# Down projection in 1024-column groups, with Strassen's seven products for seven pairs of contraction tiles

## The chip, the cores and the metric

The kernel runs on one core of one Trainium2 chip. The metric is the device time of one execution in microseconds, lower is better. The time before is 1343.54 us, the median of three runs (1343.22 to 1344.33). Engine names in the profile: PE is TensorE (matmul), PEld its weight load, DVE is VectorE, ACT is ScalarE, POOL is GpSimd, SP is SyncE, which issues most loads.

## The reference

One layer of an encoder trunk over 256 positions of width 2048, float32: a parallel mixer (gated MLP and neighbourhood attention), then a convolutional gated MLP, then a final norm. The change touches only the last matrix product of the MLP and what follows it:

```python
D_MODEL = 2048; SEQ = 256; D_FF = 5504; RMS_EPS = 1e-6

def conv_ffn(x, g_norm, w_up, conv_k, conv_b, w_down):
    h = rms_norm(x, g_norm)
    up = h @ w_up
    ...
    gate, val = jnp.split(up, 2, axis=-1)
    return x + (jax.nn.silu(gate) * val) @ w_down

def reference(...):
    for l in range(DEPTH):
        x = mixer_block(...)
        x = conv_ffn(...)
    return rms_norm(x, norm_final)
```

The down projection multiplies 256 x 5504 activations by a 5504 x 2048 weight, 43 contraction tiles of 128.

## The kernel before

**Precision.** All large products keep float32 accuracy with a faster matmul format. Each operand is split into a high part (rounded) and a low part (the rest), and a product is three matmuls that accumulate into one PSUM bank: high x high, low x high, high x low (`products`, L198 to L200). In the down projection the activations are the stationary operand, 128 x 128, and the weights move, 512 columns at a time. The high parts are made by ScalarE (L127), the low parts by VectorE (L128).

**Pieces.** `plan` cuts every weight matrix of the kernel into pieces, in one list for the whole program. In the down projection a piece is two contraction tiles by 512 columns (512 KB), the last one of each group a single tile. Piece by piece, `begin(i)` does three things: it issues loads up to piece i + 4 (SyncE's queue, L104, into five raw tiles `wraw`); it issues the split of piece i + 3 (`split_to`; four buffers each of `whi` and `wlo`, so the split of i + 3 takes the buffers of i - 1 and waits for TensorE to have read them); and it runs the tasks that were put down for turn i with `at(i, f)`. Then the matmuls of piece i are issued. The order is written out by hand: each engine executes its instructions in the order in which this program issues them. A raw tile is free for the next load once both splits have read it.

**The down projection** runs in four groups of 512 output columns (`natural`, `run_group`). A group has 22 pieces; both blocks of 128 positions are done for each piece, 6 matmuls per block and contraction pair, 12 a piece, into two PSUM banks. When a group ends, `ev_down` adds the two banks to the residual `x2` (VectorE, L752), sums the squares (ScalarE, L753), and multiplies with the final norm's weight (VectorE, L762). The weight of the final norm, `gfin`, is loaded in four parts by GpSimd's queue (L943), two buffers. The last group does its last four pieces block by block, so that `finish` of the first block of positions (the norm factor, five scalings, five stores; L777 to L795) runs beside the second block's matmuls.

**Ahead of it** stands the up projection (`ev_up`: convolution, gate, split of the activations; L717 to L738 and L328, L329), whose last tasks fall into the first pieces of the down projection. The activations lie in 43 tiles `a0` to `a42`, the normed input of the up projection in sixteen tiles `h0` to `h15` of a pool that lives to the end.

Of the kernel before, what the change touches and what calls it, by code (L numbers as in the profile page):

```python
# [15 lines left out]
T = 256  # L16
# [23 lines left out]
LOAD_AHEAD = 5  # L40
SPLIT_AHEAD = 3
WAKE = (9, 8)


@with_exitstack
def trunk_kernel(ctx, tc, x, norm_mix, w_in, ln_g, ln_b, w_s, b_s, rpb, w_branch, w_out,
# [30 lines left out]
    def plan(src, row0, nk, blocks):  # L77
        first = len(pieces)
        for k in range(0, nk, 2):
            pieces.append((src, row0 + k * 128, min(2, nk - k), blocks))  # L80
        return first

    raw, split_t = {}, {}
    n_loaded = [0]
    n_split = [0]
    first = {}

    def load_to(n):
        while n_loaded[0] < min(n, len(pieces)):
            i = n_loaded[0]  # L90
            n_loaded[0] += 1
            if i in preload:
                for f in preload[i]:
                    f()
            src, r0, kn, (c0, cn, nb, cs) = pieces[i]
            w = wpool.tile([128, 2, 512], F32, name="wraw", bufs=LOAD_AHEAD)
            ld = src.shape[-1]
            if i == 0:
                for k in range(kn):
                    if k:  # L100
                        load_x(256, 256)
                    nc.sync.dma_start(w[:, k, :cn], src[r0 + k * 128:r0 + (k + 1) * 128, c0:c0 + cn])
            elif nb == 1:
                nc.sync.dma_start(  # L104
                    w[:, :kn, :cn],
                    bass.AP(tensor=src.tensor, offset=src.offset + r0 * ld + c0,
                            ap=[[ld, 128], [128 * ld, kn], [1, cn]]))
            else:
                for b in range(nb):
                    nc.sync.dma_start(  # L110
                        w[:, :kn, b * cn:(b + 1) * cn],
                        bass.AP(tensor=src.tensor, offset=src.offset + r0 * ld + c0 + b * cs,
                                ap=[[ld, 128], [128 * ld, kn], [1, cn]]))
            raw[i] = w

    def split_to(n):
        while n_split[0] < min(n, len(pieces)):
            i = n_split[0]
            n_split[0] += 1
            src, r0, kn, (c0, cn, nb, cs) = pieces[i]  # L120
            w = raw.pop(i)
            h = wpool.tile([128, 2, 512], F32R, name="whi", bufs=SPLIT_AHEAD + 1)
            l = wpool.tile([128, 2, 512], F32R, name="wlo", bufs=SPLIT_AHEAD + 1)
            m = cn * nb

            def part(k):
                nc.scalar.activation(h[:, k, :m], w[:, k, :m], AF.Copy)  # L127
                nc.vector.tensor_sub(l[:, k, :m], w[:, k, :m], h[:, k, :m].bitcast(F32))  # L128
# [73 lines left out]
    def run_group(g, by_block=0):  # L202
        kind, n0, nk, m, acts, done = g
        nblk = NT if kind == "nat" else m // 128
        n1 = n0 + (nk + 1) // 2
        ps = None
        for i in range(n0, n1 - by_block):
            begin(i)
            h, l = split_t.pop(i)
            if ps is None:  # L210
                ps = [bank() for _ in range(nblk)]
            if kind == "ws":
                spread_products(g, ps, i, h, l)
                continue
            for b in range(nblk):
                if b == 1 and i in midway:
                    midway.pop(i)()
                products(g, ps, i, b, h, l)
        if not by_block:
            done(ps, n1)  # L220
            return
        for b in range(nblk):
            for i in range(n1 - by_block, n1):
                if b == 0:
                    begin(i)
                products(g, ps, i, b, *split_t[i])
            done(ps, b)

    def finish_tasks():
        i = cur[0] + 1  # L230
# [100 lines left out]
    xT = [hpool.tile([128, 2, T], F32R, name=f"h{k}") for k in range(KD)]  # L331

    def x_chunk(c):
        p = bank()
# [359 lines left out]
    def turn_x2(j):  # L694
        x2 = rs["x2"]
        for k2 in range(2):
            p = bank()
            for kk in range(2):
                c = j * 4 + k2 * 2 + kk
                for t in range(NT):  # L700
                    nc.tensor.transpose(p[:, kk * T + t * 128:kk * T + (t + 1) * 128],  # L701
                                        x2[:, t, c * 128:(c + 1) * 128], ident)
            k = j * 4 + k2 * 2
            for kk in range(2):
                rs["h", k + kk] = hpool.tile([128, 2, T], F32R, name=f"h{k + kk}")
            split_pair(p, (rs["h", k], rs["h", k + 1]), gffn[:, k:k + 2])


# [37 lines left out]

    fin = {}

    def add_down(ps, t, j):
        x2 = rs["x2"]  # L750
        c = slice(j * 512, (j + 1) * 512)
        nc.vector.tensor_add(x2[:, t, c], ps[t], x2[:, t, c])  # L752
        nc.scalar.activation(junk, x2[:, t, c], AF.Square, accum_out=fin["ss"][:, t, j:j + 1])  # L753

    def ev_down(j):
        def done(ps, i):
            for t in range(NT):
                add_down(ps, t, j)
            x2 = rs["x2"]
            for t in range(NT):  # L760
                c = slice(j * 512, (j + 1) * 512)
                nc.vector.tensor_mul(x2[:, t, c], x2[:, t, c], fin["g", j])  # L762
            if j < 2:
                fin["load"]()
        return done

    def finish_start():
        fin["part"] = const.tile([128, NT], F32, name="part")
        nc.vector.tensor_reduce(fin["part"], fin["ss"][:, :, 0:3], axis=AX.X, op=OP.add)
        nc.vector.tensor_scalar(fin["part"], fin["part"], 1.0 / D, RMS_EPS, op0=OP.mult, op1=OP.add)  # L770

    def finish(ps, t):
        x2 = rs["x2"]
        last = slice(1536, 2048)
        add_down(ps, t, 3)
        y = hpool.tile([128, 512], F32, name=f"h{t}")
# [142 lines left out]
    rs["st"].close()  # L919
    fa, fa_st = pool("act")  # L920
    ctx.push(fa_st)
    ff["a"] = [fa.tile([128, 2, T], F32R, name=f"a{k}") for k in range(NF)]
    fc = {}

    def open_conv():
# [18 lines left out]
                                                 ap=[[0, 128], [1, 512]]))  # L944

    fin["load"] = load_fin
    at(g_dn[3][1], sqrt_ready)
    at(g_dn[3][1] + 2, finish_start)
    for g in g_dn[:3]:
        run_group(g)  # L950
    run_group(g_dn[3], SPLIT_AHEAD + 1)
    finish_tasks()


# [26 lines left out]
```

## Time and profile before

| | |
|---|---|
| median of three runs | 1343.54 us |
| profiled execution | 1342.71 us, span 1340.8 us |
| TensorE busy | 1329.1 us, 99% of the span |
| VectorE busy | 871.2 us, 65% |
| ScalarE busy | 718.6 us, 54% |
| loads of the down weight | 84 of 512 KB and 4 of 256 KB, medians 4.6 and 3.3 us to landing |
| granted TensorE clock, mean | 0.998 |

The span runs from the first to the last instruction. In rows of groups come line, engine, operation, out<-in, shape and count, then after the bar the busy time in us and the mean of one in ns, then the idle time of that engine ahead of these instructions and what ended it. In rows of the timeline come the start and the duration in us, and in brackets the idle time ahead and what ended it; "x2" means that two instructions were merged in the row. Matmuls overlap: the duration of one is its latency, and the pace has to be read from starts. In rows of waits come the total, the number and the longest.

### The profile page before, as it was taken

The page shows a single profiled execution, that of the slowest core. Times are in us where ns is not written, and L with a number is a line of the kernel's source. Part 1 is how long each engine was busy: PE and PEld are TensorE (multiplying, and loading weights), DVE is VectorE, ACT ScalarE, POOL GpSimd, SP SyncE. Part 2 cuts the span into 40 slices and gives each one's busy share as a digit, 9 for nine tenths or more (in the row PEclk, how much of TensorE's full clock was granted, in tenths as well). Part 3 has the DMA queues.
Part 4 walks back from the last instruction along what each step waited for, and adds up shares of the span by engine and source line. Part 5 has one row for each costly group of instructions (what it writes and reads, how often), then busy time and mean ns, then how long its engine had stood idle before and what let it go on. Part 6 is the DMA issues. An engine that isn't in the chain of part 4 may idle for free.

```text
span 1340.8 us, 18983 instructions
## 1 busy us (share of the span) xinstructions
PE 1329.1 (99%) x6863; PEld 1128.8 (84%) x6863; DVE 871.2 (65%) x1256; ACT 718.6 (54%) x1059; POOL 104.4 (8%) x192
## 2 busy tenths in 40 slices
PE   9999999999999999999999999999999999999997
PEld 7888888888888888888888888888888888888885
DVE  6486667766564545555777777777777785545454
ACT  6655566667544444455655555555555554434342
POOL 0241055530000000000000000000000000000000
PEclk9999999999999999999999999999999999999999
DMA  9766685654666666665565656665665557666662
GB/s 328 224 191 177 202 232 172 193 172 157 204 187 189 190 189 220 204 203 185 178 196 181 193 184 191 187 189 188 188 190 187 174 175 227 210 184 210 187 200 100
DMA packets 194030, 259.36 MB, mean 193 GB/s; under 512 B 12952, under 2 KB 124432, under 8 KB 193936
## 3 DMA queue, kind: packets, MB, share of 16 engines
q1 hardware_dynamic: 189648, 250.31, 59.6%
q0 software_dynamic: 3968, 7.30, 2.3%
q8 instruction: 54, 0.88, 0.3%
q10 hardware_dynamic: 320, 0.53, 0.1%
q14 instruction: 40, 0.33, 0.1%
HBM read 253.90 MB, written 2.10 MB: 191 GB/s over the span
## 4 chain that ended last, share of the span: by engine, by line
PE 98%; ACT 1%; DVE 0%; DMA 0%; issue 0%; SPq 0%; DVEq 0%; ACTq 0%
PE bank L177 30%; PE bank L198 17%; PE bank L200 17%; PE bank L199 17%; PE bank L181 15%; PE bank L563 1%; DMA wraw<-in_w_in_dram 0%; PE bank L613 0%; PE bank L439 0%; PE bank L659 0%; PE bank L603 0%; PE bank L701 0%; PE bank L338 0%; ACT L634 0%; DVE x L791 0%
## 5 line engine op out<-in xcount | busy, mean ns | idle before, releaser
L128 DVE TENSOR_TENSOR wlo<-wraw,whi 128x1024 fp32r<-128x1024 f32 (+1 forms) x473 | 570.6, 1211 | 397.0 <-ACT whi L127 381.5
L127 ACT ACTIVATE whi<-wraw 128x1024 fp32r<-128x1024 f32 (+1 forms) x473 | 491.4, 1044 | 411.0 <-PE bank L199 279.8
L177 PE MATMUL bank<-h,whi 128*128 128x512 f32 x1760 | 478.6, 395 | 0.0
L177 PEld LDWEIGHTS bank<-h,whi 128*128 128x128 f32 x1760 | 302.2, 189 | 41.5
L181 PEld LDWEIGHTS bank<-h,wlo 128*128 128x128 f32 x1760 | 267.2, 189 | 35.7
L181 PE MATMUL bank<-h,wlo 128*128 128x256 f32 x1760 | 276.7, 281 | 0.0
L198 PE MATMUL bank<-whi,h 128*128 128x512 f32 x384 | 152.5, 397 | 0.1
L199 PE MATMUL bank<-whi,h 128*128 128x512 f32 x384 | 149.9, 390 | 0.3 <-DVE h L325 0.3
L200 PE MATMUL bank<-wlo,h 128*128 128x512 f32 x384 | 150.0, 391 | 0.0
L199 PE MATMUL bank<-whi,a 128*128 128x512 f32 x344 | 133.8, 389 | 0.0
L200 PE MATMUL bank<-wlo,a 128*128 128x512 f32 x344 | 133.8, 389 | 0.0
L198 PE MATMUL bank<-whi,a 128*128 128x512 f32 x344 | 133.8, 389 | 0.0
L200 PEld LDWEIGHTS bank<-wlo,h 128*128 128x128 f32 x384 | 72.2, 188 | 15.7 <-DVE wlo L128 0.4
L199 PEld LDWEIGHTS bank<-whi,h 128*128 128x128 f32 x384 | 72.3, 188 | 14.8 <-DVE h L325 0.6
L198 PEld LDWEIGHTS bank<-whi,h 128*128 128x128 f32 x384 | 72.3, 188 | 14.8 <-ACT whi L127 0.7
L727 ACT ACTIVATE tc<-ta,ck 128x256 f32<-128x256 f32 x86 | 47.1, 595 | 69.8 <-DVE ta L725 69.8
L200 PEld LDWEIGHTS bank<-wlo,a 128*128 128x128 f32 x344 | 64.6, 188 | 13.5
L199 PEld LDWEIGHTS bank<-whi,a 128*128 128x128 f32 x344 | 64.6, 188 | 13.4
L198 PEld LDWEIGHTS bank<-whi,a 128*128 128x128 f32 x344 | 64.6, 188 | 13.3
L943 POOL DMA_DIRECT2D gfin<-in_norm_final_dram x4 | 2.2, 548 | 646.5 <-DVE tc L738 539.2
L730 DVE SCALAR_TENSOR_TENSOR tc<-ta,ck,tc 128x255 f32<-128x255 f32 x86 | 41.4, 481 | 14.4 <-ACT tc L727 14.4
L198 PE MATMUL bank<-whi,m 128*128 128x512 f32 x128 | 50.1, 392 | 0.0
(157 smaller groups left out, 1093.8 us busy)
## 6 DMA issues: line engine op xcount, KB each, us to landing
wraw<-in_w_up_dram SPq DMA_DIRECT2D x336, 256.0 KB, 3.2
wraw<-in_w_in_dram SPq DMA_DIRECT2D x111, 512.0 KB, 4.3
wraw<-in_w_down_dram SPq DMA_DIRECT2D x84, 512.0 KB, 4.6
wraw<-in_w_in_dram SPq DMA_DIRECT2D x66, 256.0 KB, 3.1
wraw<-in_w_branch_dram SPq DMA_DIRECT2D x32, 512.0 KB, 4.5
wraw<-in_w_out_dram SPq DMA_DIRECT2D x32, 512.0 KB, 3.9
xs<-in_x_dram SPq DMA_DIRECT2D x8, 256.0 KB, 7.4
vw<-va POOLq DMA_DIRECT2D x32, 64.0 KB, 5.4
```

Source lines behind the costliest of these rows:

```text
L127: nc.scalar.activation(h[:, k, :m], w[:, k, :m], AF.Copy)
L128: nc.vector.tensor_sub(l[:, k, :m], w[:, k, :m], h[:, k, :m].bitcast(F32))
L177: nc.tensor.matmul(p, h[:, k - k0, b * 128:(b + 1) * 128], acts(k), start=k == 0, stop=k == nk - 1)
L181: nc.tensor.matmul(p[:, :T], l[:, k - k0, b * 128:(b + 1) * 128], acts(k)[:, 0, :], start=False, stop=False)
L198: nc.tensor.matmul(p, xh, h[:, kk, :m], start=st, stop=False)
L199: nc.tensor.matmul(p, xl, h[:, kk, :m], start=False, stop=False)
L200: nc.tensor.matmul(p, xh, l[:, kk, :m], start=False, stop=sp)
L563: nc.tensor.matmul(o, Q[s][:, c], k.rearrange("p (r c) -> p r c", r=ROWS)[:, :, k0:k0 + UNION], start=n == 0, stop=n == 1)
L727: nc.scalar.activation(v, u, AF.Identity, scale=ck[:, 1, ch:ch + 1], bias=ck[:, 3, ch:ch + 1])
L730: nc.vector.scalar_tensor_tensor(v[:, 1:], u[:, :T - 1], ck[:, 0, ch:ch + 1], v[:, 1:], op0=OP.mult, op1=OP.add)
L943: nc.gpsimd.dma_start(fin["g", j], bass.AP(tensor=norm_final.tensor, offset=norm_final.offset + j * 512, ap=[[0, 128], [1, 512]]))
```

## The change

The down projection is done in two groups of 1024 columns. A piece is now one contraction tile by 1024 columns (`plan_wide`), 43 pieces a group, still 512 KB and 12 matmuls (two position blocks x two column halves x three). Four PSUM banks hold a group's outputs (C).

Seven pairs of contraction tiles in each group (`DOWN_QUADS`) are done otherwise. Such a pair is a product of 2 x 2 blocks: position blocks x contraction tiles, times contraction tiles x column halves. It takes seven block products instead of eight: three of them use sums of weights and sums of activations, one uses a sum of activations, one a sum of weights. Three of the seven go into the outputs directly; four are gathered over all seven pairs in four further PSUM banks (P) and are added to the outputs once, at the end of the group's pairs (`ev_sums`).

For a pair whose pieces are i and i + 1 the tasks are:

- at turn i - 3, `act_sums`: VectorE forms float32 activations from high and low (512 columns) and four sums over 128 columns each; ScalarE copies them as high parts, VectorE takes the low parts;
- at turn i - 2, `weight_sums`: four sums over 512 columns from the raw weights, on VectorE;
- at turn i - 1, `weight_sums_split`: two splits over 1024 columns, on ScalarE and VectorE.

The ordinary split of piece i covers only its first 512 columns. The sums lie in the pool of `h`, whose sixteen tiles become eight of double size, with one buffer each; the activations `a` are laid in pairs too.

At the end of group one, `ev_down` adds four banks, and the columns of the final norm are multiplied at the next two turns. The last group does its last four pieces in four steps, by position block and column half; `finish` now also adds the first half's columns and multiplies them.

```diff
+DOWN_QUADS = (2, 5, 7, 10, 12, 15, 17)
...
-            if i:
+            if i in whole:
+                whole[i] = w
+                part(slice(0, units[i]))
+            elif i:
                 part(slice(0, kn))
...
+    def triple(p, x, h, l, st, sp):
+        xh, xl = x
+        nc.tensor.matmul(p, xh, h, start=st, stop=False)
+        nc.tensor.matmul(p, xl, h, start=False, stop=False)
+        nc.tensor.matmul(p, xh, l, start=False, stop=sp)
+
+    def act_sums(g, q, box):
+        a = g[4](q)
+        w = hpool.tile([128, 2, 512], F32, name="h6")
+        f = w[:, 0].rearrange("p (k t) -> p k t", k=2)
+        nc.vector.tensor_add(f, a[:, :, 0, :].bitcast(F32), a[:, :, 1, :].bitcast(F32))
+        s1, s2, s3, s4 = (w[:, 1, n * 128:(n + 1) * 128] for n in range(4))
+        nc.vector.tensor_add(s1, f[:, 0, 128:], f[:, 1, 128:])
+        nc.vector.tensor_sub(s3, f[:, 0, :128], f[:, 0, 128:])
+        nc.vector.tensor_sub(s2, s1, f[:, 0, :128])
+        nc.vector.tensor_sub(s4, f[:, 1, :128], s2)
+        o = hpool.tile([128, 2, 512], F32R, name="h7")
+        nc.scalar.activation(o[:, 0], w[:, 1], AF.Copy)
+        nc.vector.tensor_sub(o[:, 1], w[:, 1], o[:, 0].bitcast(F32))
...
+
+    def weight_sums(i, box):
+        r0, r1 = whole.pop(i), whole.pop(i + 1)
+        t13 = hpool.tile([128, 2, 512], F32, name="h0")
+        t24 = hpool.tile([128, 2, 512], F32, name="h1")
+        nc.vector.tensor_sub(t13[:, 0], r0[:, 1], r0[:, 0])
+        nc.vector.tensor_sub(t24[:, 0], r1[:, 1], t13[:, 0])
+        nc.vector.tensor_sub(t13[:, 1], r1[:, 1], r0[:, 1])
+        nc.vector.tensor_sub(t24[:, 1], r1[:, 0], t24[:, 0])
+        box["w"] = (t13, t24)
+
+    def weight_sums_split(box):
+        u = []
+        for n, t in enumerate(box.pop("w")):
+            h = hpool.tile([128, 2, 512], F32R, name=f"h{2 + n}")
+            l = hpool.tile([128, 2, 512], F32R, name=f"h{4 + n}")
+            nc.scalar.activation(h, t, AF.Copy)
+            nc.vector.tensor_sub(l, t, h.bitcast(F32))
+            u.append((h, l))
...
+        for q in quads:
+            i, b = n0 + 2 * q, boxes.setdefault(q, {})
+            at(i - 3, lambda q=q, b=b: act_sums(g, q, b))
+            at(i - 2, lambda i=i, b=b: weight_sums(i, b))
+            at(i - 1, lambda b=b: weight_sums_split(b))
...
+            if r == 0:
+                (h0, l0), (h1, l1) = split_t[i], split_t[i + 1]
+                triple(P[0], x_of(k, 0), h0[:, 0], l0[:, 0], st, sp)
+                triple(C[0][0], x_of(k + 1, 0), h1[:, 0], l1[:, 0], False, False)
+                triple(C[0][1], boxes[q]["s"][3], h1[:, 1], l1[:, 1], False, False)
...
+            S, W = boxes[q]["s"], boxes[q]["t"]
+            triple(P[1], S[0], *W[1], st, sp)
+            triple(P[3], S[2], *W[3], st, sp)
+            triple(P[2], S[1], *W[2], st, sp)
+            triple(C[1][0], x_of(k, 1), *W[4], False, False)
+            if sp:
+                done[0](P, i)
...
+            def first_half():
+                ...
+                nc.scalar.activation(ab[:, 0], p1, AF.Copy)
+                nc.vector.tensor_add(x11, p1, x11)
+                nc.vector.tensor_add(ab[:, 1], p6, ab[:, 0])
+                nc.vector.tensor_add(m["v"], p5, ab[:, 1])
+                nc.vector.tensor_add(m["u3"], p7, ab[:, 1])
+                m["w"] = ab[:, 0]
+                nc.vector.tensor_add(m["w"], p5, m["u3"])
+
+            def second_half():
+                nc.vector.tensor_add(x12, x12, m["v"])
+                nc.vector.tensor_add(x21, x21, m["u3"])
+                nc.vector.tensor_add(x22, x22, m["w"])
...
-    g_dn = [natural(w_d, 0, NF, j * 512, 512, lambda k: ff["a"][k], ev_down(j) if j < 3 else finish) for j in range(4)]
+    g_dn = [wide(w_d, 0, NF, g * 1024, lambda k: ff["a"][k], lambda q: ff["ap"][q], DOWN_QUADS,
+                 (ev_sums(2 * g), ev_down if g == 0 else finish)) for g in range(2)]
...
+    run_wide(g_dn[0], False)
+    run_wide(g_dn[1], True, SPLIT_AHEAD + 1)
```

More of the change, by code (lines that the diff above doesn't have):

```diff
@@ L79, in plan, with plan_wide @@
         for k in range(0, nk, 2):
-            pieces.append((src, row0 + k * 128, min(2, nk - k), blocks))
+            pieces.append((src, row0 + k * 128, min(2, nk - k), blocks, 128 * src.shape[-1]))
+        return first
+    def plan_wide(src, row0, nk, c0):
+        first = len(pieces)
+        for k in range(nk):
+            pieces.append((src, row0 + k * 128, 2, (c0, 512, 1, 0), 512))
         return first
     raw, split_t = {}, {}
+    whole, units = {}, {}
     n_loaded = [0]
@@ L227, in run_group, with wide @@
             done(ps, b)
+    def wide(src, row0, nk, c0, acts, pair, quads, done):
+        n0 = plan_wide(src, row0, nk, c0)
+        for q in quads:
+            i = n0 + 2 * q
+            whole[i] = whole[i + 1] = None
+            units[i], units[i + 1] = 1, 2
+        return ("wide", n0, nk, acts, pair, quads, done)
+    def triple(p, x, h, l, st, sp):
[3 more added lines that the diff above has]
+        nc.tensor.matmul(p, xh, l, start=False, stop=sp)
@@ L763, in done, with finish @@
-            if j < 2:
-                fin["load"]()
-        return done
+                scale_columns(t, j)
+            fin["load"]()
+        for j in range(2):
+            at(i + 1 + j, lambda j=j: columns(j))
     def finish_start():
         fin["part"] = const.tile([128, NT], F32, name="part")
-        nc.vector.tensor_reduce(fin["part"], fin["ss"][:, :, 0:3], axis=AX.X, op=OP.add)
+        nc.vector.tensor_reduce(fin["part"], fin["ss"][:, :, 0:2], axis=AX.X, op=OP.add)
         nc.vector.tensor_scalar(fin["part"], fin["part"], 1.0 / D, RMS_EPS, op0=OP.mult, op1=OP.add)
-    def finish(ps, t):
+    def finish(ps, t, c):
```

112 lines of the change are left out of this document (89 added, 23 removed).

## The prediction

> **What bounds the kernel now.** I read the head of the page first, then its chain that ended last, then the groups of the down projection, the table of stretches over that stage, and last the timeline of single queues there.
>
> ```profile
> span 1340.8 us, 18983 instructions
> PE 1329.1 (99%) x6863; PEld 1128.8 (84%) x6863; DVE 871.2 (65%) x1256; ACT 718.6 (54%) x1059; POOL 104.4 (8%) x192
> PE 98%; ACT 1%; DVE 0%; DMA 0%; issue 0%; SPq 0%; DVEq 0%; ACTq 0%
> ```
>
> TensorE makes 98% of the chain, so a matmul taken away is worth its pace, as long as every other engine keeps up. The down projection stands at the end:
>
> ```profile
> 1097.84 0.39 PE L198 MATMUL bank<-whi,a 128*128 128x512 f32 x1
> 1331.55 0.39 PE L200 MATMUL bank<-wlo,a 128*128 128x512 f32 x1
> L198 PE MATMUL bank<-whi,a 128*128 128x512 f32 x344 | 133.8, 389 | 0.0
> 1134.20:1161.40 27.20, 27.20 (x122) 22.52 (x121) 14.12 (x14) 11.45 (x15) 0.54 (x1) 1.00 0.58 183
> ```
>
> The first two lines are the first and the last of 3 x 344 = 1032 matmuls: 233.71 us for 1031 steps, 0.2267 us each; the 389 ns of the group are latency, not pace. The last line is one stretch of ten pieces (columns: length, then busy time of PE, PEld, DVE, ACT, POOL, granted clock, DMA share, GB/s): PE is full at clock 1.00, VectorE busy 14.1 of 27.2 us, ScalarE 11.5. A piece is 12 matmuls, 2.72 us. What paces the other two queues:
>
> ```profile
> 1228.38 1.06 ACT L127 ACTIVATE whi<-wraw 128x1024 fp32r<-128x1024 f32 x1 [1.66 <-PE bank L199]
> 1229.48 1.23 DVE L128 TENSOR_TENSOR wlo<-wraw,whi 128x1024 fp32r<-128x1024 f32 x1 [1.49 <-ACT whi L127]
> ```
>
> ScalarE's split of a piece waits 1.66 us for TensorE's last read of the piece whose buffer it takes (four buffers: piece j+3 takes that of j-1), and VectorE waits for ScalarE. So VectorE cannot build up more lead than these buffers. That is what the change meets.
>
> **The change, part by part.** Durations for the new work:
>
> ```profile
> L128 DVE TENSOR_TENSOR wlo<-wraw,whi 128x1024 fp32r<-128x1024 f32 x79 | 96.6, 1226 | 102.5 <-ACT whi L127 102.2
> L762 DVE TENSOR_TENSOR x<-x,gfin 128x512 f32<-128x512 f32 x6 | 4.2, 692 | 0.8 <-ACT junk L753 0.6
> L738 DVE TENSOR_TENSOR tc<-tc 128x256 f32<-128x256 f32 x1 | 0.4, 421 | 0.0
> L783 DVE TENSOR_SCALAR e<-e 128x1 f32<-128x1 f32 x2 | 0.3, 155 | 0.1
> L752 DVE TENSOR_TENSOR x<-bank,x 128x512 f32<-128x512 f32 x8 | 5.2, 685 | 4.1 <-PE bank L200 4.1
> L127 ACT ACTIVATE whi<-wraw 128x1024 fp32r<-128x1024 f32 x79 | 83.4, 1059 | 111.1 <-PE bank L199 111.1
> L127 ACT ACTIVATE whi<-wraw 128x512 fp32r<-128x512 f32 x4 | 2.5, 632 | 6.6 <-PE bank L199 6.6
> 1102.90 2.36 DVE L128 TENSOR_TENSOR wlo<-wraw,whi 128x1024 fp32r<-128x1024 f32 x2
> 1101.74 2.01 ACT L127 ACTIVATE whi<-wraw 128x1024 fp32r<-128x1024 f32 x2
> 1098.38 0.48 DVE L730 SCALAR_TENSOR_TENSOR tc<-ta,ck,tc 128x255 f32<-128x255 f32 x1
> 1098.89 0.48 DVE L732 SCALAR_TENSOR_TENSOR tc<-ta,ck,tc 128x255 f32<-128x255 f32 x1
> ```
>
> Two independent VectorE splits take 2.36 us, not 2 x 1.226: each occupies the queue 0.09 us less than its duration, so 1.14 us for 1024 columns and 0.60 for 512. On ScalarE it is 0.10 (2.01 against 2 x 1.06). An op that needs the one before starts 0.03 after its end (1098.38 + 0.48 to 1098.89). Between engines I take 0.04 (ScalarE's 1228.38 + 1.06 to VectorE's 1229.48). The trace has no plain add or subtract over 128 columns; its bounds are 155 ns (one column) and 421 (256). I take 0.285, the line through 256 and 512 columns (0.421 - 0.136).
>
> The Trainium skill, VectorE: DVE Perf Modes, section The DRAIN you can't avoid, says that after a VectorE op the next one does not start until the pipeline is empty. The 2.36 us above disagree. By that rule there would be no 0.09 to save; the sum would be that of rival B.
>
> *Products.* A quad is two pieces, i and i+1, that are computed by seven products of three matmuls each. Fourteen quads (seven a group, two groups) do 21 matmuls each instead of 24: 42 fewer x 0.2267 = -9.5 us. All of it is on the path.
>
> *VectorE's list for one quad*, queue time, in the order that it is issued: the half split of piece i, 0.60; the sums of activations, 0.73 + 0.20 + 0.20 + 0.32 + 0.32 = 1.77 with the hand-over, then ScalarE's copy 0.63 + 0.04 while VectorE stands, then their low part; behind that copy on ScalarE stands the split of piece i+1 (1.06 us), so VectorE's half of it starts 3.40 after the first sum; 1.14 for it; four sums of weights 0.73 + 3 x 0.60 = 2.53; their two splits 2 x 1.14 = 2.28. Together 0.60 + 3.40 + 1.14 + 2.53 + 2.28 = 9.95 us, against 2.28 for two pieces before. Each plain piece stays 1.14.
>
> *Against TensorE.* Quads begin 4 or 6 pieces apart. Four apart: TensorE has 45 matmuls, 10.20 us; VectorE 9.95 + 2.28 = 12.23: TensorE stands 2.03 us. Six apart: 69 matmuls, 15.64, against 14.51: 1.1 to spare, which cannot be banked, since VectorE then waits for a buffer. From that buffer (TensorE's end of piece i-4, 0.19 until seen) to the first low weights: 0.19 + 0.67 + 0.60 + 3.40 + 1.14 + 2.53 + 1.14 (split of i+2) + 1.27 = 10.94 us; TensorE gets there after 47 matmuls, 10.65: it stands 0.3 to 0.4. So each pair of quads costs 2.4 us, three pairs a group, two groups: 14.4.
>
> *First quad of each group.* It is like six apart, 0.4, but VectorE comes to it late. In group one, with the tail of the up projection:
>
> ```profile
> 1096.37 0.75 DVE L725 TENSOR_TENSOR ta<-ta,rb 128x256 f32<-128x256 f32 x2
> 1099.29 1.22 DVE L128 TENSOR_TENSOR wlo<-wraw,whi 128x1024 fp32r<-128x1024 f32 x1
> 1100.43 0.42 DVE L738 TENSOR_TENSOR tc<-tc 128x256 f32<-128x256 f32 x1
> 1100.76 1.22 DVE L128 TENSOR_TENSOR wlo<-wraw,whi 128x1024 fp32r<-128x1024 f32 x1
> ```
>
> One convolution holds VectorE from 1096.37 to 1099.29, 2.9 us, gate and split 0.33 each: 3.6, in all 4.0. In group two four evictions and four multiplications, 8 x 0.60 = 4.8, in all 5.2 (ScalarE's squares lie beside). Sum of stalls 14.4 + 9.2 = 23.6 us.
>
> *Sums out of PSUM* (five of 0.685 and three of 0.692 a group, and a copy on ScalarE): at nothing. They come in the last seven or eight plain pieces, where VectorE has 2.72 - 1.14 = 1.6 us to spare each. Without that cover 2 x 5 = 10 us.
>
> *Wait for the old sums.* Four apart, ScalarE's copy into the sums' tile also waits until TensorE has read the old ones, and the split of i+1 and VectorE's half of it stand behind. Laid out as above, TensorE is done 2.7 us before; nothing.
>
> *Loads and banks.*
>
> ```profile
> wraw<-in_w_down_dram SPq DMA_DIRECT2D x84, 512.0 KB, 4.6
> wraw<-in_w_down_dram SPq DMA_DIRECT2D x4, 256.0 KB, 3.3
> SPq L104 <- DVE wlo L128: 165.2, 75, 3.9
> ```
>
> SyncE's queue issues 86 loads instead of 84 + 4. It waits for VectorE to free a raw tile before nearly each load (75 times in this stage, 3.9 us at most), and will go on doing so. A quad's two raw tiles are held until the weight sums, two pieces longer, and the load that takes their place starts then; it lands 4.6 us later, near the end of piece i+1, when the split asks for it. Up to 0.1 a quad, taken as nothing. All eight PSUM banks are in use; group two's product banks were group one's output banks, evicted 10 us before their first matmul; nothing. GpSimd's two late loads of the final weights have some 100 us (40 pieces). ScalarE gets 0.63 + 2 x 1.06 more a quad and a half split less, 7 x 2.3 = 16 us a group, and is busy 11.5 of 27.2 us now: not a bound by itself, only by its order behind the copy.
>
> *Tail.*
>
> ```profile
> 1327.21 0.69 DVE L752 TENSOR_TENSOR x<-bank,x 128x512 f32<-128x512 f32 x1 [3.63 <-PE bank L200]
> 1327.94 0.63 ACT L753 ACTIVATE junk<-x 128x512 f32<-128x512 f32 x1 [5.08 <-DVE x L752]
> 1331.00 0.55 DVE L791 TENSOR_SCALAR x<-h,r,e 128x512 f32<-128x512 f32 x1
> 1331.97 0.69 DVE L752 TENSOR_TENSOR x<-bank,x 128x512 f32<-128x512 f32 x1 [0.42 <-PE bank L200]
> ```
>
> The finish of the first row block holds VectorE 4.3 us (1327.21 to 1331.55). Now another block's add, square, multiplication and small op (0.72 + 0.67 + 0.60 + 0.2, about 2.2) come behind it, before the last add: 6.5 us after, while TensorE ends after 24 matmuls, 5.4: +1.0.
>
> **Sum:** -9.5 + 23.6 + 1.0 = +15.1 us. The profiled execution took 1342.71 (span 1340.8 and 1.9 around it), 0.8 under the median of the three runs, 1343.54. Against it 1357.8, against the median 1358.6, which I give.
>
> **Rivals.** *A, the new work hides, faster.* If VectorE's list of a quad took 10.20 - 2.28 = 7.9 us or less, not 9.95, TensorE would hardly stand: -9.5 + 1.0, 1335.0. For it: VectorE is half idle on average. Against: even without both stands for ScalarE (1.1 us) the list is 8.9, and its rows are of the same shapes.
>
> *B, VectorE ops don't overlap.* 24 ops of each ten pieces lose 0.09 us: 2.2 x 6 pairs, +13, 1372. Against: the 2.36 us.
>
> *C, the clock falls in the stalls.* At its start the kernel shows slow matmuls:
>
> ```profile
> 7.11 0.63 PE L199 MATMUL bank<-whi,h 128*128 128x512 f32 x1
> 7.53 0.48 PE L200 MATMUL bank<-wlo,h 128*128 128x512 f32 x1
> ```
>
> 0.42 us apart, not 0.227. If both first quads, where TensorE stands 4 to 5 us with pauses, led to 15 such matmuls each, +5.8, 1364.4. Against: the single stands are 1.3 to 2.9 us. The Trainium skill, TensorE: Matmul & The Clock Gate, Part 1, has the clock halved after an idle window of about 3.4 us; no run here shows such a window, and by it a single stand would not do.
>
> *D, the spare time is banked.* If VectorE kept the 1.1 us of the six-apart stretches, a pair would cost 0.9: stalls 5.4 + 9.2, in all +6.1, 1349.6. Against: the 1.66 us wait for the buffer.
>
> **Chances.** Forecast 0.72, A 0.08, B 0.07, C 0.05, D 0.08. The 128-column ops alone move the sum: at 0.155 the four take 0.5 us less a quad, 14 x 0.5 = 7 down; at 0.42 as much up. With D and hand-overs shorter by 0.02 the low end is 1346; B gives the high end, 1372. A stays outside. Within 0.2% of before (2.7 us, about what a measurement can tell): 0.02, from D with cheap sums; faster 0.08, A; slower 0.90.
>
> **What would show it.** PE's matmuls of the stage: 990 at an unchanged 389 ns. The first use of the summed weights should wait for their high and low parts, 2 us in quads four apart, 0.4 in six, 4 to 5 in first ones; TensorE otherwise waits for nothing. VectorE is over 90% busy from piece 1 to 36 of each group, granted clock 1.00. If VectorE idles there for buffers, A holds; a row of two splits in 2.45 us shows B.

## The result, and the profile after

The changed kernel takes 1366.38 us, the median of four runs (1363.70 to 1366.78); the kernel before, beside it, 1343.38 (1342.94 to 1344.33). The ratio is 1.0166, with a 95% interval of 1.0154 to 1.0179: 23.0 us slower. The profiled execution took 1366.30, span 1364.3, against 1340.8 before: 23.5 us to explain.

The head of its page, the granted clock by slices, the chain that ended last, and the loads of the down weight:

```profile
span 1364.3 us, 19137 instructions
PE 1332.9 (98%) x6821; PEld 1123.4 (82%) x6821; DVE 967.6 (71%) x1440; ACT 744.6 (55%) x1101; POOL 104.5 (8%) x192
...
PEclk9999999999999999999999999999999989998999
...
PE 90%; DVE 6%; ACT 2%; issue 1%; DMA 0%; SPq 0%; ACTq 0%; DVEq 0%
...
wraw<-in_w_down_dram SPq DMA_DIRECT2D x86, 512.0 KB, 5.3
```

Forty-two matmuls are gone (6863 before, 6821 now), yet TensorE is busy 3.8 us longer. Eight points of the chain that were TensorE's are now VectorE's, ScalarE's and "issue". Two slices of the clock row have an 8, where the row of before has a 9 throughout. So there are two things to look for: places where TensorE stands, and matmuls that are themselves slow.

TensorE in the timeline (start, duration, then the idle time ahead and what ended it): the first and last matmul of the stage, the first quad of group one, one pair of stands four pieces apart, and the first wait of group two:

```profile
1098.95 0.39 PE L253 MATMUL bank<-whi,a 128*128 128x512 f32 x1
...
1112.06 0.50 PE L253 MATMUL bank<-whi,a 128*128 128x512 f32 x1 [1.38 <-ACT whi L135]
...
1113.32 0.50 PE L255 MATMUL bank<-wlo,a 128*128 128x512 f32 x1 [0.53 <-DVE wlo L136]
...
1116.34 0.79 PE L253 MATMUL bank<-h,h 128*128 128x512 f32 x1 [1.83 <-ACT h L287]
...
1118.45 0.80 PE L255 MATMUL bank<-h,h 128*128 128x512 f32 x1 [0.90 <-DVE h L288]
...
1122.87 0.40 PE L253 MATMUL bank<-whi,a 128*128 128x512 f32 x1
...
1146.89 0.50 PE L253 MATMUL bank<-h,h 128*128 128x512 f32 x1 [0.48 <-ACT h L287]
...
1148.61 0.50 PE L255 MATMUL bank<-h,h 128*128 128x512 f32 x1 [0.99 <-DVE h L288]
...
1242.38 0.79 PE L253 MATMUL bank<-h,h 128*128 128x512 f32 x1 [2.91 <-ACT h L287]
...
1353.82 0.39 PE L255 MATMUL bank<-wlo,a 128*128 128x512 f32 x1
```

The stage has 990 matmuls and lasts 254.87 us from the first start to the last, against 233.71 for 1032 before: +21.16. At the old pace 989 steps would take 224.2, so 30.7 us are lost. I took each step between two starts and put down what it has above 0.2267 us to the place where it stands. Between 1118.45 and 1122.87 no matmul waits, but ten steps take 4.42 us instead of 2.27; the first takes 0.60 us and the others 0.41 to 0.43 each. Told apart in this way, standing and slow matmuls make:

| where (group one, group two) | lost | of it slow matmuls |
|---|---|---|
| first quad of group one | 8.3 | 2.0 |
| first quad of group two | 6.8 | 2.3 |
| six quads four apart | 2.01, 2.02, 2.06, 2.06, 2.07, 3.65 | 1.6 in the last figure |
| six quads six apart | 0.17 to 0.19 each, 1.1 in all | none |
| all else | 0.6 | none |

Against that stand 42 x 0.2267 = 9.5 us saved. From the start of the last matmul to the end of the span it is 10.49 us instead of 9.22: +1.3. The stage began 1.1 us later (1098.95 against 1097.84). Matched matmul by matmul, the two traces are already 1.1 us apart from about 207 us on, 890 us ahead of the stage; and in the profiles of the experiments the stage begins anywhere from 1097.95 to 1099.39: it is spread between executions. 21.16 + 1.27 + 1.11 = 23.5.

Windows of the stage (columns as in the prediction: length, busy time of PE, PEld, DVE, ACT, POOL, granted clock, DMA share, GB/s):

```profile
1108.00:1118.00 10.00, 5.82 (x20) 3.35 (x18) 8.91 (x16) 5.60 (x8) 0.57 (x1) 0.90 0.20 67
1118.00:1128.00 10.00, 9.54 (x33) 7.73 (x34) 7.00 (x11) 3.01 (x4) 0.55 (x1) 0.76 0.96 304
1139.07:1167.23 28.16, 26.69 (x116) 21.16 (x115) 24.64 (x35) 14.14 (x16) 0.00 (x0) 1.00 0.59 202
...
1298.00:1308.00 10.00, 8.48 (x30) 6.19 (x29) 9.49 (x12) 4.96 (x5) 0.00 (x0) 0.83 0.61 186
```

The second line is the plain case of "busy but slow": TensorE 9.54 us busy, 33 matmuls instead of 44, clock 0.76. The third is VectorE's cycle of ten pieces with two quads. It lasts 28.16 us, while TensorE has 114 matmuls in it (10 x 12, less 2 x 3), 25.84 us at the old pace.

What VectorE does in that cycle, with the last convolution of the up projection and the first sum of group one ahead of it, and the tail behind it:

```profile
1105.74 0.75 DVE L857 TENSOR_TENSOR ta<-ta,rb 128x256 f32<-128x256 f32 x2
...
1108.66 0.68 DVE L261 TENSOR_TENSOR h<-a 128x512 f32<-128x512 f32 x1
...
1141.58 0.69 DVE L269 TENSOR_TENSOR h<-h,h 128x512 fp32r<-128x512 f32 x1 [0.78 <-ACT h L268]
1142.53 1.23 DVE L136 TENSOR_TENSOR wlo<-wraw,whi 128x1024 fp32r<-128x1024 f32 x1 [0.26 <-ACT whi L135]
...
1147.34 2.35 DVE L288 TENSOR_TENSOR h<-h,h 128x1024 fp32r<-128x1024 f32 x2
...
1154.41 0.69 DVE L136 TENSOR_TENSOR wlo<-wraw,whi 128x512 fp32r<-128x512 f32 x1 [1.31 <-ACT whi L135]
...
1353.11 0.68 DVE L884 TENSOR_TENSOR x<-bank,x 128x512 f32<-128x512 f32 x1
...
1355.32 0.68 DVE L884 TENSOR_TENSOR x<-bank,x 128x512 f32<-128x512 f32 x1
```

VectorE stands 0.78 + 0.26 us in a quad behind ScalarE's copy, and 1.31 us once in this cycle because the split it needs waits for a buffer. The rest is a full list. Groups and waits of the stage:

```profile
L269 DVE TENSOR_TENSOR h<-h,h 128x512 fp32r<-128x512 f32 x14 | 9.7, 693 | 10.3 <-ACT h L268 10.3
...
L253 PE MATMUL bank<-whi,a 128*128 128x512 f32 x260 | 101.8, 392 | 1.4 <-ACT whi L135 1.4
...
L263 DVE TENSOR_TENSOR h<-h 128x128 f32<-128x128 f32 x14 | 4.1, 292 | 0.5
```

```profile
PE bank L253 <- ACT h L287: 7.8, 8, 2.9
PE bank L255 <- DVE h L288: 7.4, 8, 1.0
```

TensorE's sixteen waits for summed weights make 15.2 us: eight for the high parts, and after each of these one for the low parts, in the two first quads and the six quads four apart.

### The profile page after: what moved, and what is told of

It is laid out like the page before. It is cut to its first block, busy times and chain, and to the rows that moved or that the text cites. A ratio compares the mean times of both kernels' runs of the same rounds, so it can differ in the third digit from the quotient of the medians.

```text
span 1364.3 us, 19137 instructions
## 1 busy us (share of the span) xinstructions
PE 1332.9 (98%) x6821; PEld 1123.4 (82%) x6821; DVE 967.6 (71%) x1440; ACT 744.6 (55%) x1101; POOL 104.5 (8%) x192
## 4 chain that ended last, share of the span: by engine, by line
PE 90%; DVE 6%; ACT 2%; issue 1%; DMA 0%; SPq 0%; ACTq 0%; DVEq 0%
PE bank L188 30%; PE bank L192 15%; PE bank L209 10%; PE bank L211 10%; PE bank L210 10%; PE bank L255 4%; PE bank L253 4%; PE bank L254 4%; DVE wlo L136 2%; ACT whi L135 1%; DVE h L288 1%; PE bank L696 1%; DVE h L277 0%; DVE h L279 0%; DMA wraw<-in_w_in_dram 0%
## 5 line engine op out<-in xcount | busy, mean ns | idle before, releaser
L136 DVE TENSOR_TENSOR wlo<-wraw,whi 128x1024 fp32r<-128x1024 f32 (+1 forms) x471 | 560.3, 1198 | 315.0 <-ACT whi L135 301.1
L135 ACT ACTIVATE whi<-wraw 128x1024 fp32r<-128x1024 f32 (+1 forms) x471 | 482.0, 1033 | 341.9 <-PE bank L210 164.0
L253 PE MATMUL bank<-whi,a 128*128 128x512 f32 x260 | 101.8, 392 | 1.4 <-ACT whi L135 1.4
L255 PE MATMUL bank<-wlo,a 128*128 128x512 f32 x260 | 101.3, 390 | 0.5 <-DVE wlo L136 0.5
L254 PE MATMUL bank<-whi,a 128*128 128x512 f32 x260 | 101.4, 390 | 0.0
L209 PEld LDWEIGHTS bank<-whi,h 128*128 128x128 f32 x384 | 72.3, 188 | 15.1 <-ACT whi L135 0.9
L253 PEld LDWEIGHTS bank<-whi,a 128*128 128x128 f32 x260 | 49.2, 189 | 12.1 <-ACT whi L135 1.8
L255 PEld LDWEIGHTS bank<-wlo,a 128*128 128x128 f32 x260 | 49.0, 189 | 11.4 <-DVE wlo L136 1.1
L254 PEld LDWEIGHTS bank<-whi,a 128*128 128x128 f32 x260 | 49.1, 189 | 10.3
```

The lines of the kernel that those rows point to most:

```text
L209: nc.tensor.matmul(p, xh, h[:, kk, :m], start=st, stop=False)
L253: nc.tensor.matmul(p, xh, h, start=st, stop=False)
L254: nc.tensor.matmul(p, xl, h, start=False, stop=False)
L255: nc.tensor.matmul(p, xh, l, start=False, stop=sp)
```

## The experiments

All edits are against the changed kernel; the kernel before was run beside each. My theory was that VectorE's list is too long for quads four apart and for a first quad that starts too early, that six apart it fits, and that slow matmuls add some us. The rivals were that the regrouping itself costs, that something else than VectorE's order makes TensorE stand, or that the slow clock is the main loss.

### Regrouping alone

```diff
-DOWN_QUADS = (2, 5, 7, 10, 12, 15, 17)
+DOWN_QUADS = ()
```

> 1024-column groups and the new tail, but no quad: 1032 matmuls, all eight products. Theory (VectorE's list of the quads is what costs, and the clock after it): the regrouping itself costs only the tail, +1.2 us, so 1344.6; granted clock 1.00, no stand of TensorE in the stage. Rival (the regrouping, its loads or its banks cost a part of the +23 us): over +2 us, up to +10.

1344.48 us (1344.23 to 1345.47, ten runs) beside 1343.40: ratio 1.0010, 1.0000 to 1.0019. The stage lasts 233.73 us, 0.02 from before, and the time from the last matmul's start to the end is 10.50 us, 1.3 more than before. So the wider pieces and four output banks cost only the tail, about 1 us; everything else comes from the quads.

### Quads six apart only

```diff
-DOWN_QUADS = (2, 5, 7, 10, 12, 15, 17)
+DOWN_QUADS = (5, 8, 11, 14, 17)
```

> Five quads a group, all six pieces apart, the first at piece 10: 30 matmuls fewer. Theory (distance against VectorE's list decides, and a late start makes the first quad like the others): -6.8 for products, +0.2 for each of ten quads, +1.2 for the tail, clock 1.00: -3.6, about 1339.8. Rival (every quad costs about the same, 30.7 us of excess over 14 quads, 2.2 each): -6.8 + 22 + 1.2 = +16, about 1359.8.

1340.54 us (1339.54 to 1341.82, ten runs): ratio 0.9979, 0.9970 to 0.9988, faster than both kernels. In the profile the ten quads lose 0.17 to 0.19 us each, and no matmul of the stage waits. A stretch of its group one:

```profile
1120.00:1160.00 40.00, 40.00 (x176) 32.48 (x174) 34.33 (x48) 21.88 (x24) 0.00 (x0) 1.00 0.56 187
```

TensorE is full at clock 1.00 while VectorE is busy 34.3 of 40 us. Seven products instead of eight do pay here: 30 matmuls fewer make -6.8, the quads' 2.0 and the tail's 1.3 go off, which leaves -3.5; measured -2.9.

### Four apart, without the first quads

```diff
-DOWN_QUADS = (2, 5, 7, 10, 12, 15, 17)
+DOWN_QUADS = (5, 7, 10, 12, 15, 17)
```

> The quad that comes first in each group is left out, the other six stay (4 and 6 pieces apart, the first at piece 10). Theory (only the distance counts, 2.05 us four apart, 0.17 six apart or first when VectorE has caught up): -8.2 for 36 products fewer, 2 x (3 x 2.05 + 3 x 0.17) = 13.3, tail 1.2: +6.3, and up to +9 where the clock falls in a stand of 2 us: 1349.7 to 1352.4. Rival (2.2 us a quad): +19, 1362.6.

1353.81 us (1350.71 to 1355.77, four runs): ratio 1.0070, 1.0052 to 1.0088. In the profiled run, 1355.59, the six quads four apart lose 2.07 three times and 3.65 to 3.68 three times; the six others 0.18 to 0.19. The difference of 1.6 is the clock. First the stands of one of the three, in the timeline, then the window around it:

```profile
1195.61 0.50 PE L253 MATMUL bank<-h,h 128*128 128x512 f32 x1 [0.53 <-ACT h L287]
...
1197.33 0.50 PE L255 MATMUL bank<-h,h 128*128 128x512 f32 x1 [0.99 <-DVE h L288]
```

```profile
1195.00:1205.00 10.00, 8.48 (x30) 6.46 (x30) 9.93 (x11) 5.79 (x7) 0.00 (x0) 0.83 0.88 251
```

These stands are those of the quads that keep the clock (0.48 and 0.99 at 1146.89 and 1148.61 above). The medians give the same prices as the steps: against the kernel six apart this one has two quads more (-1.4) and is 13.3 slower, so six quads four apart cost 14.6, 2.4 each, falls included. And the changed kernel is this one with two first quads more: 12.6 slower and -1.4 for their products, so the two cost 13.9; the steps of the profile say 15.1. The four runs of this kernel spread over 5 us, and the mean granted clock with them (0.998 in the fastest, 0.994 in the slowest), so the number of quads that lose the clock seems to differ between executions.

### All six apart, but an early first quad

```diff
-DOWN_QUADS = (2, 5, 7, 10, 12, 15, 17)
+DOWN_QUADS = (2, 5, 8, 11, 14, 17)
```

> Six quads a group, all six pieces apart, but the first at piece 4 as in the changed kernel. Theory (the first quad meets VectorE's work left from the stage before, and TensorE's clock falls there): -8.2, first quads 8.2 + 6.8 as measured, ten others 0.17, tail 1.2: +9.7, 1353. Rival (first quads cost little when no quad follows four apart): 1340.5 or less.

1353.43 us (1352.73 to 1354.59, four runs): ratio 1.0075, 1.0060 to 1.0090. The first quads lose 7.8 and 6.1 us, the ten others 0.17 to 0.20. So a first quad costs this much by where it stands; it doesn't need the crowded quads behind it. The stand at the first quad of group two is that of the changed kernel, and what happens to the clock there is a little different:

```profile
1236.49 0.50 PE L253 MATMUL bank<-h,h 128*128 128x512 f32 x1 [2.91 <-ACT h L287]
1236.83 0.40 PE L254 MATMUL bank<-h,h 128*128 128x512 f32 x1
1238.28 0.80 PE L255 MATMUL bank<-h,h 128*128 128x512 f32 x1 [1.05 <-DVE h L288]
```

After 2.91 us of standing the matmul takes 0.50 us here and the slow ones follow the next stand; in the changed kernel, after the same 2.91 us, it takes 0.79 and the clock is low already.

### TensorE kept awake in the first quads

```diff
+    zero = const.tile([128, 128], F32R, name="zero")
+    nc.vector.memset(zero.bitcast(F32), 0.0)
+
+    def fill(p, x, n):
+        for _ in range(n):
+            nc.tensor.matmul(p[:, :T], zero, x, start=False, stop=False)
...
+                if st and not products_first:
+                    fill(C[0][0], acts(k)[:, 0, :], 8)
                 triple(C[0][0], x_of(k + 1, 0), h1[:, 0], l1[:, 0], False, False)
...
+            if st:
+                fill(C[0][0], acts(k)[:, 0, :], 22 if products_first else 14)
             triple(P[1], S[0], *W[1], st, sp)
```

> In the first quad of each group small matmuls with a stationary operand of zeros, 8 + 14 in group one and 22 in group two, run where TensorE stands; they add zeros to an output bank. Theory (the clock falls because TensorE stands): the granted clock stays 1.00 there, matmuls of the sums take 0.39 and not 0.63 us, 1.8 + 2.3 = 4 us less: about 1362.4. Rival (those matmuls are slow because their operands lie in tiles that ScalarE and VectorE write): no change, 1366.4 or a little more.

1364.50 us (1362.33 to 1365.94, four runs): ratio 1.0157, 1.0142 to 1.0172. The profiled run took 1362.33. Its stage lasts 250.49 us, 4.4 less than that of the changed kernel, which answers to the 2.0 and 2.3 us of slow matmuls in the table. The first quad of group one:

```profile
1110.44 1.12 PE L298 MATMUL bank<-a,zero 128*128 128x256 f32 x8
...
1114.26 1.84 PE L298 MATMUL bank<-a,zero 128*128 128x256 f32 x14
1116.25 0.51 PE L253 MATMUL bank<-h,h 128*128 128x512 f32 x1 [0.15 <-ACT h L287]
...
1118.37 0.50 PE L255 MATMUL bank<-h,h 128*128 128x512 f32 x1 [1.39 <-DVE h L288]
```

The window behind it, where the changed kernel had 33 matmuls at clock 0.76:

```profile
1118.00:1128.00 10.00, 9.63 (x42) 8.00 (x43) 8.17 (x13) 4.54 (x6) 0.55 (x1) 1.00 0.94 313
```

The summed weights come at the same moments (1116.25 and 1118.37, against 1116.34 and 1118.45), so the list is what it was; but the matmuls behind them are at full pace at once, 0.39 to 0.40 us each, at clock 1.00. So the slow matmuls are a loss of their own, caused by the standing, and worth some 4 us of the 23 by the profiles. They are not the main loss. The medians say less, 1.9 us, and the intervals of the two kernels overlap (1.0142 to 1.0172 here, 1.0154 to 1.0179 for the changed kernel), so the runs alone would not show a gain. At one quad four apart the clock still fell in this profile (3.63 us lost there); that quad had no filling, and the mean granted clock of the four runs goes from 0.993 to 0.996.

### Sums of weights on GpSimd

```diff
-        nc.vector.tensor_sub(t13[:, 0], r0[:, 1], r0[:, 0])
+        nc.gpsimd.tensor_sub(t13[:, 0], r0[:, 1], r0[:, 0])
```

and so the three below it.

> The four sums of weights run on GpSimd. Theory (VectorE's list is too long by 2 us four apart): the list falls by 2.5 to 7.4 us, under 7.9, so quads four apart no longer stand; first quads keep some 4 and 2 us; -9.5 + 1.2 + 6 + 1 = -1.3, about 1342. Rival (GpSimd is slow, or VectorE slows down beside it): sums later than VectorE's own, 1355 to 1370; the durations of VectorE's ops beside GpSimd's show which.

1376.51 us (1376.13 to 1377.55, four runs): ratio 1.0247, 1.0229 to 1.0264. Taking 2.5 us a quad off VectorE's list made it slower by another 10 us. Groups of its stage:

```profile
L276 POOL TENSOR_TENSOR h<-wraw 128x512 f32<-128x512 f32 x14 | 27.6, 1970 | 608.4 <-DMA wraw<-in_w_down_dram 568.2 <-DVE h L288 40.2
...
L136 DVE TENSOR_TENSOR wlo<-wraw,whi 128x512 fp32r<-128x512 f32 x14 | 22.8, 1630 | 3.4 <-ACT whi L135 3.4
...
L261 DVE TENSOR_TENSOR h<-a 128x512 f32<-128x512 f32 x14 | 21.6, 1540 | 0.0
```

A sum takes 1.65 to 1.97 us on GpSimd on average (L276 to L279), which its queue, nearly empty in this stage, could have borne. But VectorE's own operations beside it grow: the sum of 512 columns at L261 from 0.68 to 1.54 on average, the half split from 0.69 to 1.63. TensorE's two largest waits in the stage:

```profile
PE bank L253 <- ACT whi L135: 14.3, 7, 5.3
PE bank L253 <- ACT h L287: 5.8, 1, 5.8
```

Seven waits, 14.3 us, are for the ordinary split of a piece, which stands on ScalarE behind the copy of the activation sums, and so behind VectorE's late list. One, 5.8 us at the first quad of group two, is for summed weights that came late from GpSimd itself. So most of what was taken off the list came back in the price of the rest. The Trainium skill, GPSIMD Engine Reference, section Specifications, states that GpSimd's SBUF interfaces are shared with VectorE and contend with VectorE instructions that have two SBUF inputs. Both of these have two, and the rows agree.

### Sums only once

The sums are formed for the first quad of group one, and all quads use these; thirteen quads' sums and splits are left out.

```diff
+    once = {}
...
-            i, b = n0 + 2 * q, boxes.setdefault(q, {})
+            i, b = n0 + 2 * q, boxes.setdefault(q, once)
+            if q > quads[0] or products_first:
+                continue
```

> All fourteen quads do their seven products, but the sums of weights and activations are made for the first one alone and used by all others; the sums of thirteen quads are left out. Theory (the products cost their 21 matmuls at full pace, all stands come from making the sums): excess only in group one's first quad, 8.2 with its clock; -9.5 + 8.2 + 1.2: about 1343.3, and nothing in group two. Rival (the products themselves run slower, by their operands or by going round eight banks): excess in the other quads stays, over 1350.

1343.71 us (1342.30 to 1344.03, ten runs): ratio 1.0001, 0.9992 to 1.0010. TensorE stands in one place, the first quad of group one, and loses 8.5 us there, its slow matmuls with it. The thirteen other quads run their 21 matmuls at full pace. This shows that nothing in the seven products themselves, in their banks or in the sums out of PSUM costs time: it is the making of the sums. It doesn't test the loads that are held back, since no raw tile is kept for a sum here; in the changed kernel no wait of TensorE is for a load, and ScalarE waits for one twice, 0.17 us each.

### The activations' copy moved behind the split

Now VectorE doesn't stand behind ScalarE's copy: the copy and the low part of the activation sums are issued one piece later, behind the split of piece i + 1.

```diff
+        box["f"] = w
+
+    def act_sums_split(box):
+        w = box.pop("f")
         o = hpool.tile([128, 2, 512], F32R, name="h7")
         nc.scalar.activation(o[:, 0], w[:, 1], AF.Copy)
...
+            at(i - 2, lambda b=b: act_sums_split(b))
             at(i - 2, lambda i=i, b=b: weight_sums(i, b))
```

> The copy and the low part of the activation sums come one turn later, behind the split of piece i+1, so that VectorE no longer stands for ScalarE: 1.06 us less in its list, no work less. Theory (TensorE stands for as long as VectorE's list is longer than TensorE's time between quads): four apart 2.05 falls to 1.0, first quads by 1 us each: -8, 1358, and less of the clock's fall. Rival (the stand is the latency of the last sums or of loads, not the list): 1366.

1352.52 us (1351.91 to 1353.01, four runs): ratio 1.0068, 1.0053 to 1.0083. That is 13.9 us less than the changed kernel, by order alone, with the same instructions. The quads four apart lose 0.75 to 0.78 us instead of 2.05, those six apart nothing; the first quads 7.0 and 5.0. One quad of the four-apart kind in TensorE's timeline:

```profile
1144.23 0.39 PE L254 MATMUL bank<-h,h 128*128 128x512 f32 x1
1145.10 0.50 PE L255 MATMUL bank<-h,h 128*128 128x512 f32 x1 [0.47 <-DVE h L292]
1145.43 0.40 PE L253 MATMUL bank<-h,h 128*128 128x512 f32 x1
```

The wait for the high parts is gone, and no matmul is slow at any of the six. I had counted on the 1.06 us by which the list is shorter; the quads gained 1.3, and with the falls of the clock at these quads gone and less lost at the first ones (3.1 us in the profiles), the whole came out better than forecast.

### Both, and a sixth quad

Six apart, with the later copy, and with two more of the final scalings of the first row block on ScalarE, to shorten the tail:

```diff
-DOWN_QUADS = (2, 5, 7, 10, 12, 15, 17)
+DOWN_QUADS = (5, 8, 11, 14, 17)
...
-            if n == 2:
+            if n == 2 or t == 0 and n in (1, 3):
                 nc.scalar.activation(v, u, AF.Copy, scale=both)
```

> Five quads a group, six pieces apart, first at piece 10, with the later copy and low part of the activation sums; in the tail ScalarE takes two more scalings of the first position block (0.74 us off VectorE's list there). Theory: -6.8 for 30 products, no stand at the quads (0.17 each goes too), tail +0.3 to +0.5 instead of +1.2: -6.2, about 1337.1. Rival (0.17 and the tail are not on VectorE's list): as the six-apart kernel before it, 1340.5.

1339.21 us (1338.39 to 1339.74, six runs): ratio 0.9970, 0.9959 to 0.9982, the lowest median here, though the interval overlaps those of the two other kernels with five or six quads six apart. The stage loses 1.0 us in all, 0.8 of it in one quad; but the tail is 10.43 us as ever. ScalarE and VectorE in its last microseconds:

```profile
1325.53 1.74 ACT L964 ACTIVATE x<-x,b 128x512 f32<-128x512 f32 x3 [1.19 <-DVE b L968]
...
1327.31 0.63 ACT L890 ACTIVATE junk<-x 128x512 f32<-128x512 f32 x1
...
1328.07 0.69 DVE L922 TENSOR_TENSOR x<-x,gfin 128x512 f32<-128x512 f32 x1 [1.52 <-ACT junk L890]
```

The square of the second position block's first half (1327.31) stands behind the three scalings on ScalarE, and VectorE waits 1.52 us for it, where it waits 0.79 in the changed kernel: the work that I took off one queue I put in front of what that queue waits for.

The second kernel has the same edits, and six quads in group two, the first at piece 6 and the last at piece 36, two pieces later than in group one:

```diff
-DOWN_QUADS = (2, 5, 7, 10, 12, 15, 17)
+DOWN_QUADS = ((5, 8, 11, 14, 17), (3, 6, 9, 12, 15, 18))
...
```

> The same with a sixth quad in group two, the first at piece 6. Theory (VectorE catches up 1.6 us a plain piece, so at piece 6 it is late by some 3 us less than at piece 4, where group two stood 3.3 us without its clock): -7.5 for 33 products, 0.3 to 1 us at that first quad, no fall of the clock, tail as before: -6.0 to -6.7, 1336.6 to 1337.4. Rival (any early quad costs its whole stand and the clock): 1341 or more.

1339.79 us (1339.18 to 1340.47, ten runs): ratio 0.9975, 0.9965 to 0.9984. The three matmuls saved (0.7 us) don't show. In the profile the stage loses 1.9 us instead of 1.0, of which 1.3 at one plain piece near the end (1319.18) that waits for its split, and the tail is 11.01 instead of 10.43. Both stand behind the sums out of PSUM, which come 4.2 us later in this kernel, since its last quad is two pieces later (the first sum at 1314.66 instead of 1310.44):

```profile
1314.66 0.69 DVE L904 TENSOR_TENSOR x<-bank,x 128x512 f32<-128x512 f32 x1
...
1317.91 1.22 DVE L136 TENSOR_TENSOR wlo<-wraw,whi 128x1024 fp32r<-128x1024 f32 x1
...
1320.85 0.69 DVE L889 TENSOR_TENSOR x<-bank,x 128x512 f32<-128x512 f32 x1
```

The split at 1317.91 is the one that TensorE waits for, and VectorE comes to the first position block's banks at 1320.85 instead of 1319.61. No run moves these sums alone.

More buffers for the splits, or keeping the activation sums from group one for group two, were not tried.

## Why the prediction was right, and where it was not

The direction and the mechanism held, and the size was 8 us too small: 1358.6 against 1366.4, within the range given. That the range reaches so far is in part luck: its upper end, 1372, was priced for rival B, which did not happen, and what filled it was rival C and a mis-sized first quad.

One row of before matters for the first quads. It is VectorE's second convolution of the up projection in the stage, behind the rows that the prediction quotes:

```profile
1105.16 0.76 DVE L725 TENSOR_TENSOR ta<-ta,rb 128x256 f32<-128x256 f32 x2
```

By its steps, against the profiled execution (+15.1 forecast, +23.5 measured):

- **Products, -9.5:** held. 42 matmuls are gone, and at 0.2267 us the table closes.
- **VectorE's list:** held. A cycle of two quads was to take TensorE's 10.20 + 2.03 and 15.64 + 0.3 to 0.4, 28.2 us; it takes 28.16. The stand of 1.04 us behind ScalarE is in the rows (0.78 + 0.26), and the 128-column operations, which no row of before had, take 0.28 to 0.29 (my 0.285).
- **Four apart, 2.03:** held; 2.01 to 2.07, where the clock stayed.
- **Six apart, 0.3 to 0.4:** too much; 0.17 to 0.19, which is 1.1 less in all.
- **First quads, 4.0 and 5.2:** mis-sized in group one, by 2.3 us. Without slow matmuls they are 6.3 and 4.5. I put one convolution of the up projection ahead of the sums, but two lie there: the second starts at 1105.74 and takes 2.9 us, and VectorE comes to the first sum at 1108.66, 9.7 us into the stage, where my terms put it at about 7 (2.72 + 0.19 + 0.67 + 0.60 + 2.9). The trace of before has both, one inside the rows that I quoted and one behind them (the row above); I should have followed VectorE's queue to the turn at which the sums are issued.
- **Rival C, the clock:** this is the step that failed. I gave it 0.05 and nothing in the sum, because the single stands were to be 1.3 to 2.9 us, and by the window of some 3.4 us that the Trainium skill states (TensorE: Matmul & The Clock Gate, Part 1) a single stand would not do. The stands were that long, the longest 2.91 us, and the clock fell all the same: 4.3 us at the two first quads together, near the 5.8 that I had priced, and 1.6 at one quad four apart, where I expected none. In its profile the kernel kept awake gets the 4.3 back. So rival C came in addition to the forecast and not in its place, and 5.9 of the missing 8.4 us are its own.
- **Tail, +1.0:** 1.3. The regrouped kernel without quads shows it alone.
- **At nothing:** sums out of PSUM, banks, loads. The kernel with its sums made once shows nothing of the first two: all quads but the first run without a loss. Loads land later (5.3 us instead of 4.6), and in the changed kernel no wait of TensorE is for one; what ScalarE's two waits of 0.17 us cost no run tells.
- **Rival A:** out; the list is what I laid out. Its price, though, is right as a limit: with the sums made once, the stage without its first quad runs as A says.
- **Rival B:** out; two splits take 2.35 us, not 2.45. What the prediction took from the Trainium skill (VectorE: DVE Perf Modes, The DRAIN you can't avoid) is half of it: the same paragraph goes on that a next operation which is not held starts earlier. The 2.35 us of these independent operations agree with that half.
- **Rival D:** out; VectorE waits for a buffer in each of the six cycles of two quads, 1.27 to 1.31 us in three of them and 2.6 to 3.6 us in the three that follow a fall of the clock.
- **What would show it:** VectorE was to be over 90% busy; it is 24.64 of 28.16 us, 87%, since it stands behind ScalarE and for the buffer. The waits stood where I named them, but for two: at the first quad of group one TensorE also stood 1.38 and 0.53 us for the ordinary split of the quad's second piece (1112.06 and 1113.32 above). The granted clock was not 1.00, but 0.76 in the window behind the first quad of group one.

The other 2.5 us of the gap are the 1.1 by which this execution was late before the stage began, 0.6 spread over the stage, 0.3 of the tail, and 0.5 that is left of the first quads' +1.6 and the six-apart quads' -1.1.

## What to carry to other kernels

A trade of matmuls for vector work is decided place by place: the same quad costs 0.2 us, 2 us or 8 us, by how much of the vector engine's queue lies between the last free buffer and its first use, and the average load says nothing of it. Lay out that queue in order, from the buffer that starts it to the matmul that needs it, with what is already queued ahead; then move a wait on another engine behind independent work before taking work away (13.9 us here, without an instruction less). Where the list is still too long, space the work out: five quads a group beat seven.

## What was not expected of the hardware

- **The clock falls after short stands.** At the quads four apart two stands of 0.5 and 1.0 us within 2.2 us (1146.41 to 1148.61 in a quad that kept the clock) were followed by slow matmuls (0.427 us a step for about 3 us) at one of six quads in the changed kernel, three of six in the one without first quads, one of six with TensorE kept awake at the first quads. With one stand of 0.5 us it fell at none of six. The Trainium skill, TensorE: Matmul & The Clock Gate, Part 1, has the lower clock after an idle window of some 3.4 us, and the window free-running. The longest stand of the changed kernel is 2.91 us, so its falls come short of the first part of the rule (where the sums were on GpSimd, TensorE stood 5.3 and 5.8 us at the first quads, and the granted clock was 0.72 and 0.63 in the 10 us around them); that the same stand ends with a low clock in one kernel and not in another would fit the second. What decides it is open.
- **VectorE slows down beside GpSimd.** Operations with two inputs grew from 0.68 to 1.54 us on average while GpSimd made sums of the same kind.
